# The 8x8 blocks' substitution on GpSimd, and the v and z projections among the quarters of S5's outputs

## The chip, the cores and the metric

The kernel runs on one core of a Trainium2 chip. The metric is the device time of one execution in microseconds (us), as the median of several runs. The engines are TensorE (PE; its weight loads are listed as PEld), VectorE (DVE), ScalarE (ACT), GpSimd (POOL) and SyncE (SP), which issues the weight transfers. Each engine works through its own queue of instructions in order.

## The reference

A two-layer decoder trunk over 16 meta tokens and 256 tokens (272 columns here), model width 1024, all in float32. In each layer

```
h += 1/2 * SwiGLU(RMSNorm(h))
h += Mixer(RMSNorm(h))
h += 1/2 * SwiGLU(RMSNorm(h))
```

The mixer has one input projection whose columns go to three groups: stick-breaking attention (q, k, v, 256 columns each, 4 heads of 64), gated DeltaNet (its own qkv of 768 columns, a gate z of 256, and the small b and a), and S5 (512 columns, u).

```
o_sb = rmsnorm(stick_breaking(q, k, v)) 
o_dn = rmsnorm(chunk_gated_delta_rule(...), out_norm) * silu(z)
y    = gelu(S5 states and inputs through C, D);  y = y * sigmoid(y @ w_glu + b_glu)
o_s5 = rmsnorm(y)
out  = concatenate([o_sb, o_dn, o_s5]) @ w_out
```

The delta rule works in chunks of 64 tokens and needs, for each chunk and head, the inverse of a unit lower triangular 64 x 64 matrix (`triangular_solve` of lmat + eye against eye).

## The kernel before, in words

Activations are kept transposed: channels on the 128 partitions, tokens along the free axis. Every large product is done three times to keep float32 accuracy: values are split into a high part rounded for TensorE and a low part (`xh`, `xl` and, for weights, `wh`, `wl`), and `mm3` (lines 142 to 146) issues high x high, high x low, low x high.

Weights come in units. `weights` (line 127) starts the transfer of a unit of up to 128 x 1088 into a buffer `raw` (3 buffers), ScalarE rounds it into `wh` (line 136), and VectorE, or GpSimd where the unit's number within the mixer is in `ON_POOL` (line 47), subtracts to get `wl` (line 139). `unit` (line 1306) projects 128 columns of the mixer's input: 8 blocks of 128 rows x 3 = 24 products into one PSUM tile, which VectorE evicts with the norm factor R (`proj`, line 1361).

The mixer (line 1317) writes its steps down in the order of `ORD` (line 41), after two convolution units, the DeltaNet gates and inverse, and the four u units. The letters: c is the other four convolution units, z the z projection with its Silu and gain, s S5's scan, r the rest of DeltaNet, q the projections of q, k and v, g S5's outputs and the GLU, b the attention, m and n norms. After `ORD` come the output projection's parts in the order `WOUT`.

The order in which each engine's queue is filled is not the written order: the tile framework plans it. It simulates the program with a cost for every instruction and takes instructions that are ready by priority; `high_priority(n)` moves a step ahead by n places (`FIRST` = 4000 for DeltaNet, `SECOND` = 1500 for S5's outputs, the GLU and their norm). Buffers of one tag (PSUM tags a, b, c, d with two buffers each) are handed on in the written order. `order` adds an edge without a semaphore between two instructions of a queue; `phase` and `act` use it to keep the activations of one table set together. The sets follow each other as Silu, exp/log, Silu, Gelu with Tanh, exp/log in each mixer.

The parts that the change touches:
- `dn_inverse` (line 970) inverts the triangular blocks in levels. Nine groups of 8 x 8 blocks (`Lb`, `TT8`) are solved by forward substitution on VectorE: for j = 0 to 6 a product (line 1005) and a subtraction (line 1006) on the columns that are left, 9 x (7 - j) elements per partition, each depending on the one before. Then the result is spread to 32 x 32 (line 1008), transposed on VectorE (line 1010), and joined on TensorE in rounds of small products: px and py for 16 and 32 (lines 1016 to 1025), px and py again for 64 and 128 (lines 1033 to 1071), with VectorE and ScalarE copying in between.
- `s5` (line 802) works in four quarters: products into PSUM (pinc, tag b), rotations and two scans on VectorE, one-column memsets on GpSimd.
- `s5_outputs` (line 842) works in the same four quarters: 24 small products each into one tile pY (tag b; lines 850 and 852), and four Gelu activations of 32 partitions.
- `do_z` projects z, applies Silu, and multiplies by the DeltaNet output gain `dng` (line 1373). `dn_out` (line 1185) multiplies the DeltaNet output by it and splits the product (lines 1201, 1202).
- `sb` (line 1205) first transposes v (pvs, PSUM tag c, line 1216), then takes its score tiles pz from the same tag.

Of the kernel before, what the change touches and what calls it, by code (L numbers as in the profile page):

```python
# [39 lines left out]
SBP = 0  # L40
ORD = "czsrqgbmn"
WOUT = "SnY"
# [3 lines left out]
CONV, UORD, ZK = (0, 1, 4, 5), (0, 1, 2, 3), 0  # L46
ON_POOL = (5, 7, 10, 15, 20, 25)
NBUF = (3, 2, 3)
# [15 lines left out]
class Trunk:  # L64
    def __init__(self, ctx, tc, a, out):
        self.ctx, self.tc, self.nc, self.a, self.out = ctx, tc, tc.nc, a, out
        pool = lambda n, b, **k: ctx.enter_context(tc.tile_pool(name=n, bufs=b, **k))
        self.const = pool("const", 1)
        self.res = pool("res", 1)
        self.raw = pool("raw", NBUF[2])  # L70
        self.wsp = pool("wsp", 2)
        self.small = pool("small", 1)
        self.ps = pool("ps", 1, space=PSUM)
        self.load_ins, self.set = None, None
        self.first = []
        self.since = []
        self.nw = 0
        self.on_pool = ()
        self.blocks = (0, 4)


# [60 lines left out]
    def mm3(self, p, wh, wl, xh, xl, first, last):  # L142
        mm = self.nc.tensor.matmul
        mm(p, wh, xh, start=first, stop=False)  # L144
        mm(p, wh, xl, start=False, stop=False)  # L145
        mm(p, wl, xh, start=False, stop=last)  # L146
# [126 lines left out]
    def load_params(self, prm):  # L273
# [26 lines left out]

        for t in (self.s5g, self.bglu):
            nc.vector.tensor_scalar(t, t, 0.5, None, op0=ALU.mult)
        self.dng = g("dn_out_norm", pat="p (l b) -> p l b", l=DEPTH)
        self.sbg = g("sb_out_norm", pat="p (l b) -> p l b", l=DEPTH)
# [536 lines left out]

    def s5_outputs(self, u):

        A, PE = self.nc.scalar, self.nc.tensor
        for r in range(4):
            p = self.psum("b", "pY")
            for b in range(4):
                q = 4 * b + r
                po = p[:, b * NCH:(b + 1) * NCH]
                PE.matmul(po, self.M0[:, q, :], self.U[:, r, b, :], start=True, stop=False)  # L850
                for k in range(2):
                    PE.matmul(po, self.W2[k][:, q].rearrange("p k g c -> p (k g c)"), self.S[r][:, k, b], start=False, stop=k == 1)  # L852
            for t in range(4):
                o = u[32 * r:32 * r + 32, :, t * NCH:t * NCH + NCH]
                self.act(o, p[32 * t:32 * t + 32, :T].rearrange("p (b c) -> p b c", b=4), AF.Gelu_apprx_tanh)

# [113 lines left out]
    def dn_inverse(self):  # L970
# [213 lines left out]

    def dn_out(self, zg, slot):

# [5 lines left out]
        for b in range(2):  # L1192
# [124 lines left out]
    def mixer(self, l, nxt):  # L1317
# [9 lines left out]
        with ExitStack() as es:  # L1327
# [32 lines left out]

            def proj(c0, dst):
                for b in range(2):
                    p, = self.unit(w_in[:, c0 + b * P:c0 + b * P + P], P)
                    V.scalar_tensor_tensor(dst[:, b, :], p[:, :T], 0.125 if c0 == 0 else 1.0, R, op0=ALU.mult, op1=ALU.mult)

            q, k, v = (tmp.tile([P, 2, T], F32, name=f"p{n}") for n in "qkv")

            def do_z():
                proj(1536, zr)
                self.phase(SET_SILU)  # L1370
                for b in range(2):
# [39 lines left out]

            steps = dict(z=do_z, s=do_s5, r=do_rest, q=do_qkv, b=do_sb, c=do_conv, g=do_glu, n=do_norm, m=do_r5)
            for x in ORD:
# [25 lines left out]
            for x in WOUT:  # L1439
                if x == "n":  # L1440
                    with first():
                        self.dn_out(zr, 2)
                    continue
# [51 lines left out]
```

## Time and profile before

| | |
|---|---|
| median of 3 runs | 1191.51 us (1189.88 to 1191.59) |
| the profiled execution | 1194.31 us |
| its span, from the first to the last instruction | 1192.5 us |
| mean granted clock of TensorE | 0.972 of full speed |
| TensorE products | 9544, busy 97% of the span |
| VectorE, ScalarE, GpSimd | busy 72%, 52%, 15% |

The rows further down are from this one execution. Times in them count from the span's start. A product's end is modelled, so products overlap in the list and a busy TensorE may still wait inside; the granted clock is 1.00 at 2.4 GHz and 0.50 at 1.2 GHz. Spans on GpSimd are rough. "Idle before" names what ended an engine's wait.

### The profile page before, as it was taken

Reading aid. Unit: us, or ns where it says so; the run is one execution under the profiler, and the core shown is the slowest. Engines: PE = TensorE matmul, PEld = TensorE weight load, DVE = VectorE, ACT = ScalarE, POOL = GpSimd, SP = SyncE. Lnnn points to the kernel's source line nnn. Section 1 sums busy time; section 2 is a strip of 40 time slices with the busy share of each in tenths; the row PEclk is TensorE's granted clock in tenths of the full one; section 3 lists DMA queues with packets and bytes.
Section 4 is the critical chain, followed back from the end, with each engine's and each line's share of the span. In section 5 each row is a group of like instructions: output and inputs, shape, how many; then the busy total and the mean of one; then the engine's idle time right before and its main releaser. Section 6 shows DMA issues by size and latency. Waiting matters only on the chain.

```text
span 1192.5 us, 23762 instructions
## 1 busy us (share of the span) xinstructions
PE 1154.8 (97%) x9544; PEld 1104.5 (93%) x9544; DVE 853.6 (72%) x1648; ACT 614.1 (52%) x981; POOL 175.3 (15%) x210
## 2 busy tenths in 40 slices
PE   8999999999998999999999999999999989999997
PEld 7999999998786999999999999999988969999985
DVE  7999986699636866555579998756994268666644
ACT  6455575564166654444455556645632566555533
POOL 6312100021010111110201112011210001111100
PEclk9999999999789999999999999999997599999999
DMA  5656545543201455555565555455431015666663
GB/s 182 179 175 180 166 135 160 167 125 108 71 19 54 142 175 177 168 176 171 177 187 177 169 173 172 132 175 156 124 112 33 27 45 185 181 188 191 187 191 117
DMA packets 196858, 173.74 MB, mean 146 GB/s; under 512 B 21300, under 2 KB 193004, under 8 KB 196748
## 3 DMA queue, kind: packets, MB, share of 16 engines
q1 hardware_dynamic: 196732, 172.22, 48.2%
q8 instruction: 75, 1.23, 0.4%
q14 instruction: 35, 0.29, 0.1%
q10 hardware_dynamic: 16, 0.00, 0.0%
HBM read 171.15 MB, written 1.05 MB: 144 GB/s over the span
## 4 chain that ended last, share of the span: by engine, by line
PE 84%; DVE 10%; ACT 3%; issue 1%; DMA 1%; SPq 0%; ACTq 0%; DVEq 0%
PE proj L146 17%; PE proj L145 17%; PE proj L144 17%; PE pd L146 5%; PE pd L145 5%; PE pd L144 5%; PE pd L493 5%; DVE wl L139 2%; PE pY L852 1%; DVE qkv L1346 1%; DVE xT L1437 1%; PE pY L850 1%; PE pl L887 1%; PE pm L783 1%; PE pz L1227 1%
## 5 line engine op out<-in xcount | busy, mean ns | idle before, releaser
L144 PE MATMUL proj<-xh,wh 128*128 128x272 f32 (+1 forms) x1840 | 521.1, 289 | 6.3 <-DVE sy L1435 2.8
L145 PE MATMUL proj<-xl,wh 128*128 128x272 f32 (+1 forms) x1840 | 518.4, 287 | 0.2 <-DVE xl L1296 0.2
L146 PE MATMUL proj<-xh,wl 128*128 128x272 f32 (+1 forms) x1840 | 492.8, 290 | 3.3 <-DVE wl L139 3.0
L136 ACT ACTIVATE wh<-raw 128x1024 fp32r<-128x1024 f32 (+1 forms) x324 | 338.2, 1044 | 292.8 <-PE proj L145 99.5
L139 DVE TENSOR_TENSOR wl<-raw,wh 128x1024 fp32r<-128x1024 f32 (+1 forms) x312 | 378.4, 1213 | 146.6 <-PE pd L146 60.9
L144 PEld LDWEIGHTS proj<-xh,wh 128*128 128x128 f32 x1840 | 345.4, 188 | 10.5 <-DVE sy L1435 4.1
L145 PEld LDWEIGHTS proj<-xl,wh 128*128 128x128 f32 x1840 | 345.2, 188 | 3.0 <-issue 1.5
L146 PEld LDWEIGHTS proj<-xh,wl 128*128 128x128 f32 x1840 | 328.8, 187 | 7.2 <-DVE wl L139 5.8
L144 PE MATMUL pd<-hh,wh 128*128 128x272 f32 x528 | 149.6, 288 | 0.0
L145 PE MATMUL pd<-hl,wh 128*128 128x272 f32 x528 | 149.3, 288 | 0.0
L435 POOL TENSOR_TENSOR hl<-h,hh 128x272 fp32r<-128x272 f32 (+1 forms) x88 | 81.1, 924 | 452.9 <-ACT hh L434 452.8
L146 PE MATMUL pd<-hh,wl 128*128 128x272 f32 x528 | 140.8, 288 | 0.2
L144 PEld LDWEIGHTS pd<-hh,wh 128*128 128x128 f32 x528 | 99.2, 188 | 0.2
L145 PEld LDWEIGHTS pd<-hl,wh 128*128 128x128 f32 x528 | 99.3, 188 | 0.1
L146 PEld LDWEIGHTS pd<-hh,wl 128*128 128x128 f32 x528 | 95.1, 188 | 1.0 <-DVE wl L139 0.9
L107 ACT ACTIVATE g<-g 128x272 f32<-128x272 f32 (+2 forms) x92 | 37.6, 415 | 68.9 <-DVE g L429 68.8
L433 DVE TENSOR_TENSOR h<-proj,g 128x272 f32<-128x272 f32 (+1 forms) x88 | 37.7, 433 | 32.9 <-PE proj L146 21.3
L434 ACT ACTIVATE hh<-h 128x272 fp32r<-128x272 f32 (+1 forms) x88 | 36.4, 419 | 47.1 <-DVE h L433 47.1
L429 DVE TENSOR_TENSOR g<-proj,R 128x272 f32<-128x272 f32 (+1 forms) x88 | 37.5, 430 | 17.8 <-PE proj L146 17.6
L139 POOL TENSOR_TENSOR wl<-raw,wh 128x1024 fp32r<-128x1024 f32 x12 | 30.7, 2557 | 110.5 <-ACT th L107 34.9
L431 DVE TENSOR_TENSOR g<-g,R 128x272 f32<-128x272 f32 (+1 forms) x88 | 37.7, 432 | 12.6 <-ACT g L107 12.3
L376 POOL TENSOR_TENSOR acc<-acc,sq 128x272 f32<-128x272 f32 (+1 forms) x20 | 22.7, 1134 | 91.4 <-ACT sq L370 90.5
(490 smaller groups left out, 1310.1 us busy)
## 6 DMA issues: line engine op xcount, KB each, us to landing
raw<-in_ffn_w_gate_dram SPq DMA_DIRECT2D x88, 512.0 KB, 3.6
raw<-in_ffn_w_up_dram SPq DMA_DIRECT2D x88, 512.0 KB, 3.6
raw<-in_ffn_w_down_dram SPq DMA_DIRECT2D x70, 512.0 KB, 3.5
raw<-in_w_in_dram SPq DMA_DIRECT2D x36, 512.0 KB, 4.4
raw<-in_ffn_w_down_dram SPq DMA_DIRECT2D x24, 384.0 KB, 3.0
raw<-in_w_out_dram SPq DMA_DIRECT2D x16, 512.0 KB, 3.5
raw<-in_s_w_glu_dram SPq DMA_DIRECT2D x4, 512.0 KB, 3.4
xin<-in_x_dram SPq DMA_DIRECT2D x4, 256.0 KB, 5.8
```

The costliest lines, as they stand in the source:

```text
L107: i = self.nc.scalar.activation(out, in_, func, **k)
L136: nc.scalar.activation(h[:, :n], r[:, :n], AF.Copy)
L139: e.tensor_tensor(l[:, :n], r[:, :n], f32(h[:, :n]), op=ALU.subtract)
L144: mm(p, wh, xh, start=first, stop=False)
L145: mm(p, wh, xl, start=False, stop=False)
L146: mm(p, wl, xh, start=False, stop=last)
L429: V.tensor_tensor(g1, pg[j][:, :N], R, op=ALU.mult)
L431: V.tensor_tensor(g1, g1, R, op=ALU.mult)
L433: V.tensor_tensor(h, pu[j][:, :N], g1, op=ALU.mult)
L434: nc.scalar.activation(hh[:, f, :N], h, AF.Copy)
L435: G.tensor_tensor(hl[:, f, :N], h, f32(hh[:, f, :N]), op=ALU.subtract)
L493: PE.matmul(pd[i][e], x[:, f, ts], w[:, 0, e * 512:e * 512 + 512], start=f == 0 and w is h and x is hh, stop=f == NF - 1 and w is lo)
```

## The change

- In the inverse the copy of the identity into `TT8`, the fourteen instructions of the substitution and the spread to 32 x 32 are issued on GpSimd instead of VectorE. The transpose behind them stays on VectorE.
- The steps z and v leave their places. z is no longer a letter of `ORD`, and `do_qkv` projects q and k only. S5's outputs are written as quarter 0, unit v0, quarter 1, unit v1, quarter 2, unit z0, quarter 3, unit z1, then the GLU. An order edge (`behind`) puts the first product of each unit behind the last product of the quarter before it; nothing binds the next quarter behind the unit but the written order.
- z's Silu becomes a Tanh of half the argument (in the Gelu set) and one VectorE instruction, (tanh + 1) * z. The missing half is put into the gain, which is halved at the start and applied in `dn_out`, as the scale of the rounding activation and in the subtraction.
- `ON_POOL` loses the numbers 10 and 15, which were the first z unit and the second k unit. The other four numbers stand for the same units as before (the last u, the second convolution of step c, the first and the last-but-two of the output projection).

```
-ORD = "czsrqgbmn"
+ORD = "csrqgbmn"
-ON_POOL = (5, 7, 10, 15, 20, 25)
+ON_POOL = (5, 7, 20, 25)
...
     def mm3(self, p, wh, wl, xh, xl, first, last):
         mm = self.nc.tensor.matmul
-        mm(p, wh, xh, start=first, stop=False)
+        i = mm(p, wh, xh, start=first, stop=False)
+        if self.behind is not None:
+            self.order(getattr(i, "ins", i), self.behind)
+            self.behind = None
...
-        for t in (self.s5g, self.bglu):
+        self.dng = g("dn_out_norm", pat="p (l b) -> p l b", l=DEPTH)
+        for t in (self.s5g, self.bglu, self.dng):
             nc.vector.tensor_scalar(t, t, 0.5, None, op0=ALU.mult)
...
-    def s5_outputs(self, u):
+    def s5_outputs(self, u, r):
...
-        V.tensor_copy(TT8, bc(self.id8, 1, 9))
+        G.tensor_copy(TT8, bc(self.id8, 1, 9))
         for j in range(7):
-            V.tensor_tensor(t8[:, :, j + 1:], Lb[:, :, j + 1:, j], TT8[:, :, j:j + 1].to_broadcast([P, 9, 7 - j]), op=ALU.mult)
-            V.tensor_tensor(TT8[:, :, j + 1:], TT8[:, :, j + 1:], t8[:, :, j + 1:], op=ALU.subtract)
+            G.tensor_tensor(t8[:, :, j + 1:], Lb[:, :, j + 1:, j], TT8[:, :, j:j + 1].to_broadcast([P, 9, 7 - j]), op=ALU.mult)
+            G.tensor_tensor(TT8[:, :, j + 1:], TT8[:, :, j + 1:], t8[:, :, j + 1:], op=ALU.subtract)
         TT32, T32 = t9("TT32"), t9("T32")
-        V.tensor_tensor(TT32.rearrange("p u (b i) -> p u b i", b=4), bc(TT8, 2, 4),
+        G.tensor_tensor(TT32.rearrange("p u (b i) -> p u b i", b=4), bc(TT8, 2, 4),
...
-            A.activation(self.xh[:, slot + b, :], y, AF.Copy)
-            V.tensor_tensor(self.xl[:, slot + b, :], y, f32(self.xh[:, slot + b, :]), op=ALU.subtract)
+            A.activation(self.xh[:, slot + b, :], y, AF.Copy, scale=g)
+            V.scalar_tensor_tensor(self.xl[:, slot + b, :], y, g, f32(self.xh[:, slot + b, :]), op0=ALU.mult, op1=ALU.subtract)
...
-            def do_z():
-                proj(1536, zr)
-                self.phase(SET_SILU)
-                for b in range(2):
-                    self.act(zr[:, b, :], zr[:, b, :], AF.Silu)
-                    V.tensor_scalar(zr[:, b, :], zr[:, b, :], self.dng[:, l], None, op0=ALU.mult)
+            def do_z(b):
+                proj(1536, zr, b)
+                t = self.cv("zt")[:, :T]
+                self.act(t, zr[:, b, :], AF.Tanh, scale=0.5)
+                V.scalar_tensor_tensor(zr[:, b, :], t, 1.0, zr[:, b, :], op0=ALU.add, op1=ALU.mult)
...
-                for c0, dst in ((0, q), (256, k), (512, v)):
-                    proj(c0, dst)
+                for c0, dst in ((0, q), (256, k)):
+                    for b in range(2):
+                        proj(c0, dst, b)
...
-                    self.s5_outputs(u)
+                    units = (proj, 512, v, 0), (proj, 512, v, 1), (do_z, 0), (do_z, 1)
+                    for r, (f, *args) in enumerate(units):
+                        self.behind = self.s5_outputs(u, r)
+                        f(*args)
                     self.acc = self.glu(l, u)
```

`s5_outputs(u, r)` is the body of the old loop for one r, and returns its last product.

## Rows read from the trace of the kernel before

**Rows 1.** The page: busy time of each engine; TensorE's clock in 40 slices.
```profile
PE 1154.8 (97%) x9544; PEld 1104.5 (93%) x9544; DVE 853.6 (72%) x1648; ACT 614.1 (52%) x981; POOL 175.3 (15%) x210
...
PEclk9999999999789999999999999999997599999999
```

**Rows 2.** Stretches: length, busy (count) of PE, PEld, DVE, ACT, POOL; PEclk, DMA share, GB/s.
```profile
265.00:308.10 43.10, 38.89 (x307) 36.42 (x305) 42.85 (x88) 16.60 (x26) 7.77 (x7) 0.99 0.41 122
...
308.10:325.00 16.90, 16.86 (x292) 13.99 (x292) 9.07 (x20) 1.06 (x4) 0.11 (x1) 0.51 0.10 33
...
325.00:341.80 16.80, 16.80 (x301) 16.24 (x295) 2.91 (x7) 7.66 (x20) 2.55 (x5) 1.00 0.01 3
...
341.80:349.70 7.90, 7.06 (x37) 6.73 (x35) 1.92 (x5) 3.33 (x10) 0.63 (x1) 0.57 0.00 0
...
357.80:389.00 31.20, 27.29 (x199) 21.01 (x200) 20.57 (x55) 18.29 (x39) 0.44 (x1) 1.00 0.16 51
...
420.00:840.00 420.00, 419.49 (x3361) 415.57 (x3360) 298.51 (x535) 218.54 (x320) 58.97 (x66) 1.00 0.57 171
...
912.30:931.20 18.90, 18.90 (x233) 18.28 (x226) 3.04 (x7) 6.94 (x18) 1.38 (x4) 0.85 0.01 2
...
931.20:949.80 18.60, 18.17 (x90) 17.24 (x90) 5.00 (x14) 8.91 (x20) 2.35 (x1) 0.51 0.09 29
...
952.40:982.00 29.60, 25.47 (x192) 19.71 (x193) 19.09 (x50) 18.41 (x39) 0.29 (x1) 1.00 0.16 54
```

**Rows 3.** VectorE by form, 265 to 308.1 us: busy us, mean ns, idle before.
```profile
L139 DVE TENSOR_TENSOR wl<-raw,wh 128x1024 fp32r<-128x1024 f32 x8 | 9.7, 1211 | 0.0
...
L1364 DVE SCALAR_TENSOR_TENSOR pz<-proj,R 128x272 f32<-128x272 f32 x2 | 0.8, 422 | 0.0
...
L1373 DVE TENSOR_SCALAR pz<-pz,prm 128x272 f32<-128x272 f32 x2 | 0.7, 342 | 0.0
...
L1008 DVE TENSOR_TENSOR TT<-TT,m8c 128x288 f32<-128x288 f32 x1 | 0.5, 452 | 0.0
```

**Rows 4.** VectorE in order of time: start, us, instruction.
```profile
265.17 2.95 DVE L1346 SCALAR_TENSOR_TENSOR qkv<-pad,prm,qkv 128x272 f32<-128x272 f32 x2
...
268.73 0.49 DVE L1346 SCALAR_TENSOR_TENSOR qkv<-pad,prm,qkv 128x272 f32<-128x272 f32 x1
...
283.46 0.23 DVE L1005 TENSOR_TENSOR t<-Lb,TT 128x63 f32<-128x63 f32 x1
...
288.08 1.64 DVE L1006 TENSOR_TENSOR TT<-TT,t 128x54 f32<-128x54 f32 x1
...
308.61 0.47 DVE L1010 STREAM_TRANSPOSE T<-TT 128x288 f32<-128x288 f32 x1
```

**Rows 5.** Line 1005 alone, 265 to 308.1 us: length, VectorE busy (count).
```profile
265.00:308.10 43.10, 1.39 (x7) 0.99 0.41 122
```

**Rows 6.** Line 1006 alone, the same stretch.
```profile
265.00:308.10 43.10, 2.74 (x7) 0.99 0.41 122
```

**Rows 7.** GpSimd in order of time: start, us, instruction.
```profile
264.91 2.37 POOL L139 TENSOR_TENSOR wl<-raw,wh 128x1024 fp32r<-128x1024 f32 x1 [3.25 <-PE proj L146]
...
273.93 2.05 POOL L1001 TENSOR_TENSOR Lm<-L,lev 128x288 f32<-128x288 f32 x2 [6.65 <-ACT qkv L1344]
...
286.55 3.10 POOL L139 TENSOR_TENSOR wl<-raw,wh 128x1024 fp32r<-128x1024 f32 x1 [1.42 <-PE proj L146]
```

**Rows 8.** Tile px in two stretches: length, busy of PE, PEld, DVE, ACT.
```profile
308.10:325.00 16.90, 2.31 (x144) 2.06 (x144) 0.00 (x0) 0.43 (x2) 0.51 0.10 33
...
325.00:341.80 16.80, 2.85 (x64) 2.59 (x64) 0.86 (x2) 1.09 (x3) 1.00 0.01 3
```

**Rows 9.** Tile py, 325 to 341.8 us: the same columns.
```profile
325.00:341.80 16.80, 2.78 (x134) 2.56 (x135) 1.30 (x3) 0.37 (x1) 1.00 0.01 3
```

**Rows 10.** Tile pz, 308.1 to 325 us: the same columns.
```profile
308.10:325.00 16.90, 4.58 (x18) 2.58 (x12) 0.00 (x0) 0.00 (x0) 0.51 0.10 33
```

**Rows 11.** Tile pY, 325 to 341.8 us: length, busy of PE, PEld, ACT.
```profile
325.00:341.80 16.80, 11.79 (x96) 11.09 (x96) 5.40 (x14) 1.00 0.01 3
```

More of the change, by code (lines that the diff above doesn't have):

```diff
@@ L143, in mm3 @@
         mm = self.nc.tensor.matmul
-        mm(p, wh, xh, start=first, stop=False)
+        i = mm(p, wh, xh, start=first, stop=False)
+        if self.behind is not None:
+            self.order(getattr(i, "ins", i), self.behind)
+            self.behind = None
         mm(p, wh, xl, start=False, stop=False)
@@ L299, in load_params @@
         self.cw = g("dn_conv_w", pat="p (l k b) -> p l k b", l=DEPTH, k=4)
-        for t in (self.s5g, self.bglu):
+        self.dng = g("dn_out_norm", pat="p (l b) -> p l b", l=DEPTH)
+        for t in (self.s5g, self.bglu, self.dng):
             nc.vector.tensor_scalar(t, t, 0.5, None, op0=ALU.mult)
-        self.dng = g("dn_out_norm", pat="p (l b) -> p l b", l=DEPTH)
         self.sbg = g("sb_out_norm", pat="p (l b) -> p l b", l=DEPTH)
@@ L840, in s5 @@
             self.S.append(z)
-    def s5_outputs(self, u):
[L844 to L855, printed above, removed]
+    def s5_outputs(self, u, r):
+        PE = self.nc.tensor
+        p = self.psum("b", "pY")
+        for b in range(4):
+            q = 4 * b + r
+            po = p[:, b * NCH:(b + 1) * NCH]
+            PE.matmul(po, self.M0[:, q, :], self.U[:, r, b, :], start=True, stop=False)
+            for k in range(2):
+                i = PE.matmul(po, self.W2[k][:, q].rearrange("p k g c -> p (k g c)"), self.S[r][:, k, b], start=False, stop=k == 1)
+        for t in range(4):
+            o = u[32 * r:32 * r + 32, :, t * NCH:t * NCH + NCH]
+            self.act(o, p[32 * t:32 * t + 32, :T].rearrange("p (b c) -> p b c", b=4), AF.Gelu_apprx_tanh)
+        return getattr(i, "ins", i)
     def dn_tile(self, sh, nm, b=1):
@@ L1183, in dn_norm, with dn_out @@
         V.tensor_tensor(o, o, bc(r, 2, 64), op=ALU.mult)
-    def dn_out(self, zg, slot):
+    def dn_out(self, zg, g, slot):
         nc = self.nc
@@ L1359, in mixer, with proj @@
             zr = tmp.tile([P, 2, T], F32, name="pz")
-            def proj(c0, dst):
-                for b in range(2):
-                    p, = self.unit(w_in[:, c0 + b * P:c0 + b * P + P], P)
-                    V.scalar_tensor_tensor(dst[:, b, :], p[:, :T], 0.125 if c0 == 0 else 1.0, R, op0=ALU.mult, op1=ALU.mult)
+            def proj(c0, dst, b):
+                p, = self.unit(w_in[:, c0 + b * P:c0 + b * P + P], P)
+                V.scalar_tensor_tensor(dst[:, b, :], p[:, :T], 0.125 if c0 == 0 else 1.0, R, op0=ALU.mult, op1=ALU.mult)
             q, k, v = (tmp.tile([P, 2, T], F32, name=f"p{n}") for n in "qkv")
-            def do_z():
-                proj(1536, zr)
-                self.phase(SET_SILU)
-                for b in range(2):
-                    self.act(zr[:, b, :], zr[:, b, :], AF.Silu)
-                    V.tensor_scalar(zr[:, b, :], zr[:, b, :], self.dng[:, l], None, op0=ALU.mult)
+            def do_z(b):
[3 more added lines that the diff above has]
+                V.scalar_tensor_tensor(zr[:, b, :], t, 1.0, zr[:, b, :], op0=ALU.add, op1=ALU.mult)
             def do_s5():
@@ L1410, in do_r5 @@
                     self.rms(self.acc, 4 * 512, 0, self.R5, "b")
-            steps = dict(z=do_z, s=do_s5, r=do_rest, q=do_qkv, b=do_sb, c=do_conv, g=do_glu, n=do_norm, m=do_r5)
+            steps = dict(s=do_s5, r=do_rest, q=do_qkv, b=do_sb, c=do_conv, g=do_glu, n=do_norm, m=do_r5)
             for x in ORD:
@@ L1441, in mixer @@
                     with first():
-                        self.dn_out(zr, 2)
+                        self.dn_out(zr, self.dng[:, l], 2)
                     continue
```

## The prediction

> **What bounds the kernel now.** I read the page first, then the two mixers by stretches, then each engine inside the stretches. On the page TensorE (PE) is busy 97% of the span, and its granted clock is full except in slices that fall in the mixers, one per layer [rows 1]. In the feed-forward stretch from 420 to 840 us there is nothing to win: 3361 products in 419.5 us at full clock, 0.125 us each, so a projection unit of 24 products costs 3.0 us [rows 2]. What can be won lies in the mixers. Layer 1's VectorE order repeats layer 0's some 588 us later, so I work layer 0 out and give layer 1's differences. Four stretches matter [rows 2]:
> S1, 265.0 to 308.1 us: VectorE is busy 42.85 of 43.1 us, TensorE stands for 4.2. VectorE is the bound.
> S2, 308.1 to 325.0: TensorE is busy throughout, but at a granted clock of 0.51, after the idle time at the end of S1; here run DeltaNet's small products, the inverse's first rounds (tiles px, py) and the attention scores (pz).
> S3, 325.0 to 341.8: TensorE is full; S5's four quarters (pY) and the rest of the inverse.
> S4, from 341.8: the GLU's products, at a clock of 0.57 over 7.9 us; in layer 1 S3 runs at 0.85 and S4 at 0.51 over 18.6 us.
> After S4's last Tanh ScalarE loads the exp/log table and the attention chain runs, 31.2 us in layer 0 and 29.6 in layer 1 [rows 2]. Its end lets the last output projection start, so time taken out before the table load is won, as long as that chain keeps its length.
>
> **The change, part by part, per layer.** Instructions on VectorE start about 0.08 us closer together than they last, so I take 0.08 off each that goes.
>
> VectorE in S1, what goes. The substitution's 14 instructions last 1.39 + 2.74 us [rows 5, 6], but one of the latter lasts 1.64 [rows 4] where its neighbours last 0.2; without that excess (1.44) they are 2.7. The initial copy is 0.2 and the masked spread 0.45 [rows 3]: 3.4 together. The excess goes too. It is a hold: the slow instruction, started at 288.08, ends at 289.72, and GpSimd's 3.10 us subtraction from 286.55 ends at 289.65 [rows 4, 7]. The other subtraction that leaves GpSimd does the same: two convolution steps take 2.95 us from 265.17, beside GpSimd's from 264.91, where one alone takes 0.49 [rows 4, 7]; 2.0 us. So 3.4 us of holds go. Three low-part subtractions (z1, v0, v1) move out, one (k1, on GpSimd before) comes in: 2 x 1.21 = 2.4. Four evictions at 0.42 and two gain multiplications at 0.34 go: 2.4 [rows 3]. Sum 11.6, less 24 x 0.08 = 1.9: 9.7 us.
>
> VectorE in S1, what comes. GpSimd's sixteen instructions (copy, 14, spread) hold VectorE whenever it reads two operands from SBUF. The nearest rows for one: 1.03 us for 288 elements and 2.37 for 1024 [rows 7], so an estimate of 0.50 fixed and 1.8 ns an element. The 14 have 504 elements together: 7.0 + 0.9 = 7.9; copy and spread make it 9.6 us. VectorE pays between nothing (when each falls beside an instruction that reads PSUM) and 9.6; I take half, 4.8, since the two rows on holds show a part of GpSimd's time held in one and nearly all in the other. Also, the substitution took from 283.46 until its transpose at 308.61 [rows 4], 25 us, because its links are scattered in VectorE's queue. On GpSimd, 16 instructions of 0.6 with a wait of about as much before each take some 19 us at most, and they start about 4 us earlier, as z's work ahead of them is gone. So the inverse begins 10 us or more earlier, and of its nine VectorE steps (0.45 each by the spread's row) more than half come into S1: 2.5. S1: -9.7 + 4.8 + 2.5 = -2.4 us, with -9.7 and +2.4 as ends. TensorE is no bound there: 38.9 us of work less four units of 3.0 leaves 27, in about 41.
>
> TensorE in S2. The inverse's first rounds (px 2.31 us [rows 8]) find room in S1's idle time, and the scores (4.58 us [rows 10]) wait now: their PSUM buffers come after v's transposes, and v comes later. -6.9.
>
> TensorE in S3. v0, v1 and z0 come in, 9.0 us. The scores follow at full clock, 2.3. Of the inverse's 2.85 + 2.78 us here [rows 8, 9] I let half go; later DeltaNet steps take the other places: -2.6. pY's 11.79 us stay [rows 11]. +8.7. ScalarE and VectorE, busy 7.7 and 2.9 of 16.8 us here [rows 2], hide the units' copies, subtractions, evictions and z's Tanh. If ScalarE's cover is gone (its Gelus stand behind copies that wait for a weight buffer), a quarter's Gelu comes up to one unit, 3.0 us, later. The weight transfers move with the units and pass nothing on SyncE's queue but the GLU's and output's weights, which come later; DMA is 1% busy in S3, so they cost nothing. The new order edge binds a unit's first product behind its quarter's last, on one queue; behind that product stand the next quarter and the GLU (through its PSUM buffers), and they wait only if the unit's low part is late, which VectorE's idle 13.9 us hide. S5's one-column memsets on GpSimd now stand among the substitution's instructions: one of 0.6 us is the most that each should wait, and pY needs them much later.
>
> S4. z1 comes in, 3.0, into the 0.84 us in which TensorE waits for the last Gelus. The quarters now alternate with dense units, so I expect full clock up to the GLU: that gives back (1 - 0.57) x 7.9 = 3.4 in layer 0, and 9.1 in S4 plus 2.8 in S3 in layer 1 [rows 2]. S4: -1.2 in layer 0; in layer 1 (gap 0.43) 2.6 - 9.1 - 2.8 = -9.3.
>
> The tail. Layer 1's attention chain is 1.6 us shorter than layer 0's, and its DeltaNet is further ahead when the table is loaded; so -1.6 in layer 0, nothing in layer 1. The gain folded into the output (two VectorE instructions and two activations with a scale) costs about 0.2: a scalar form with a per-partition operand lasts 0.49 against 0.42 [rows 3, 4]. It could be 0.5.
>
> Sum: layer 0 -2.4 - 6.9 + 8.7 - 1.2 - 1.4 = -3.2; layer 1 -2.4 - 6.9 + 8.7 - 9.3 + 0.2 = -9.7. Together -12.9 on the profiled execution's 1194.3 us, 1181.4; that execution is 2.8 above the median of 1191.5, so 1178.6, in round figures 1179.
>
> **Rivals.**
> A, more: GpSimd's instructions fall where VectorE reads PSUM (4.8 us less per layer), and TensorE runs the 10 us left of S2 at full clock (4.9 less). Fully that is -32 us; half of it, a further 10, gives 1169. For it: half of S2's low-clock products leave. Against: S2 keeps only small products, and S1 now leaves TensorE idle for some 14 us instead of 4.2 right ahead of it.
> B, the holds eat it: VectorE stands for all of GpSimd's 9.6 us; 2 x 4.8 more makes 1188. If the transpose on VectorE stands early in its queue and waits for GpSimd (behind it are S5's scans and the units' subtractions, and TensorE waits for these), another 4 us per layer makes 1196. For it: the 1.64 us row. Against: a waiting VectorE holds nothing, so GpSimd then runs freely.
> The Trainium skill ("SBUF — State Buffer", section "Who interferes with whom") states the hold as a rule: GpSimd and VectorE share one port pair under an exclusive lock, kept for a whole instruction. By that rule this rival has its full 9.6 us; the 289.65 and 289.72 us above agree with it.
> C, slower: v and z run at the low clock. Place: S3 and S4. All four units then cost 6.0 instead of 3.0 (+12 per layer), and the credits of 3.4 and 11.9 are lost: 12.9 is answered by +39.3 over both layers. It decides from a third of that on (13 us); at half, the time is 1198. For it: layer 1's S4 stayed at 0.51 through 18.6 us although the GLU's dense products fill most of it. Against: S3 came to full clock in layer 0 with pY alone.
>
> **How the numbers follow.** My forecast (1172 to 1187) gets 0.48, A 0.20, B 0.15, C 0.17. The range reaches half-way into A and to C's half: 1166 to 1197. About 0.2%, 2.4 us, is what a measurement tells from no change. Faster: all but 0.02 of the forecast, all of A, 0.07 of B: 0.73. Same: 0.01 of the forecast, 0.04 of B and 0.03 of C: 0.08. Slower: the rest, 0.19.
>
> **What would show it.** In S1: no substitution on VectorE, its instructions on GpSimd at about 0.6 us each, and VectorE instructions of 0.2 to 0.7 us stretched by as much beside them (B if most are). S5's last scan in each layer 2 to 3 us earlier; the transpose (line 1010 before) by 10 or more. TensorE's first pY about 9 us earlier than 325, and the quarters with units between them at a clock of 1.0 (C if 0.5). The GLU's products at 0.126 us apart in both layers, and the exp/log table loaded 2 us earlier in layer 0, some 10 in layer 1. The prediction is wrong if the table load of layer 0 is later than before, or if layer 1 gains no more than layer 0.

## The result, and the profile after

The changed kernel takes 1210.52 us (median of 4, 1210.11 to 1211.47) against 1190.70 us of the kernel before (median of 4): ratio 1.0172, interval 1.0152 to 1.0191. It is 20 us slower where I forecast 12 faster, and outside my range. The profiled execution took 1210.34 us, its span is 1208.5, 16.0 more than before. The ratios here and below leave out slow executions, over 1.5% above the fastest of their kernel (one of e7, three of e12, one of e13).

The page after, beside [rows 1]: TensorE's busy time rose by 10.8 us with the same 9544 products, so products got longer, not more. In the clock's row layer 0's mixer shows 8, 5 where 7, 8 stood.
```profile
PE 1165.6 (96%) x9544; PEld 1114.7 (92%) x9544; DVE 854.4 (71%) x1621; ACT 614.1 (51%) x981; POOL 181.7 (15%) x238
...
PEclk9999999998598999999999999999976989999998
```

Layer 0's mixer after by stretches, and layer 1's last three (columns as in [rows 2]); the mixer, counted from the last Newton step of its norm, starts at 234.6 and 835.1 us where it was 236.1 and 824.1.
```profile
262.00:287.00 25.00, 24.79 (x203) 23.52 (x201) 24.79 (x49) 11.89 (x19) 6.50 (x12) 1.00 0.46 127
287.00:291.30 4.30, 0.04 (x4) 0.07 (x6) 2.74 (x6) 0.00 (x0) 3.14 (x7) 0.93 0.38 122
291.30:303.30 12.00, 9.78 (x250) 9.29 (x251) 11.62 (x24) 0.80 (x2) 0.22 (x2) 0.50 0.01 3
303.30:313.40 10.10, 10.10 (x192) 8.84 (x191) 6.73 (x17) 1.17 (x3) 1.49 (x5) 0.50 0.02 4
313.40:328.50 15.10, 15.10 (x92) 14.59 (x91) 1.27 (x3) 2.29 (x6) 0.00 (x0) 0.51 0.00 0
328.50:353.80 25.30, 25.30 (x238) 24.40 (x236) 9.67 (x22) 11.50 (x25) 1.81 (x1) 1.00 0.19 63
353.80:368.60 14.80, 13.02 (x103) 10.40 (x101) 10.15 (x18) 10.12 (x21) 2.35 (x1) 1.00 0.23 72
...
914.00:926.00 12.00, 12.00 (x74) 11.70 (x71) 1.27 (x3) 2.29 (x6) 0.00 (x0) 0.52 0.00 1
926.00:953.00 27.00, 27.00 (x257) 25.95 (x255) 9.67 (x22) 11.49 (x25) 0.00 (x0) 1.00 0.20 59
953.00:967.80 14.80, 12.96 (x103) 10.38 (x101) 10.14 (x18) 10.12 (x21) 2.35 (x1) 1.00 0.23 71
```
Read them from the top. At 287 q's and k's units are through, and TensorE stands for 4.3 us: v's and z's products, which filled this place before, are gone. From 291 to 328.5 the clock is 0.50, 37 us long where the stretch at 308 to 325 was 17 [rows 2]; TensorE is busy nearly all of it. The quarters (313.4 to 353.8) take 40.4 us where 16.8 stood [rows 2]. Only while v's first unit runs does the clock come back. The GLU then has full clock in both layers, as forecast.

The product that ends the idle time, TensorE's order after:
```profile
291.26 0.97 PE L1022 MATMUL px<-T,Lm 32*32 32x32 f32 x55 [4.27 <-DVE T L1016]
```

The substitution on GpSimd, some of its sixteen, and VectorE beside it (start, us):
```profile
281.92 0.35 POOL L1011 TENSOR_TENSOR t<-Lb,TT 128x63 f32<-128x63 f32 x1 [0.15 <-ACT Lb L1002]
...
282.83 1.19 POOL L1011 TENSOR_TENSOR t<-Lb,TT 128x54 f32<-128x54 f32 x1
284.10 0.31 POOL L1012 TENSOR_TENSOR TT<-TT,t 128x54 f32<-128x54 f32 x1
...
289.82 0.79 POOL L1014 TENSOR_TENSOR TT<-TT,m8c 128x288 f32<-128x288 f32 x1
```
```profile
282.49 1.34 DVE L141 TENSOR_TENSOR wl<-raw,wh 128x1024 fp32r<-128x1024 f32 x1
...
290.64 0.48 DVE L1016 STREAM_TRANSPOSE T<-TT 128x288 f32<-128x288 f32 x1 [1.53 <-POOL TT L1014]
...
301.96 1.34 DVE L837 TENSOR_TENSOR_SCAN s5z<-dec,s5z 128x272 f32<-128x272 f32 x2
```
This part went better than I thought: 281.92 to 290.61, 0.3 us an instruction where nothing is in the way. It is GpSimd that waits: its 1.19 us instruction starts while VectorE's subtraction of 282.49 runs and ends 0.2 us after it; that subtraction is 0.13 us over the mean of [rows 3], and the most that another VectorE instruction beside the sixteen is stretched is 0.16 (the one at 281.98). The last scan ends at 303.3 (311.9 before), the transpose is at 290.64 (308.61 in [rows 4]).

ScalarE's load of the exp/log table in the two layers, which I had named as the test, before and after:
```profile
357.82 1.28 ACT L97 ACT_TABLE_LOAD   x1
...
952.45 1.28 ACT L97 ACT_TABLE_LOAD   x1
```
```profile
368.55 1.28 ACT L99 ACT_TABLE_LOAD   x1
...
967.75 1.28 ACT L99 ACT_TABLE_LOAD   x1
```
In layer 0 that is 10.7 us later than before, 12.2 counted from the mixer's start.

### The profile page after: what moved, and what is told of

It reads as the page before. It is cut to its first block, busy times and chain, and to the rows that moved or that the text cites. A ratio compares the mean times of both kernels' runs of the same rounds, so it can differ in the third digit from the quotient of the medians.

```text
span 1208.5 us, 23745 instructions
## 1 busy us (share of the span) xinstructions
PE 1165.6 (96%) x9544; PEld 1114.7 (92%) x9544; DVE 854.4 (71%) x1621; ACT 614.1 (51%) x981; POOL 181.7 (15%) x238
## 4 chain that ended last, share of the span: by engine, by line
PE 88%; DVE 6%; ACT 3%; POOL 1%; issue 1%; DMA 1%; SPq 0%; ACTq 0%; DVEq 0%; POOLq 0%
PE proj L151 18%; PE proj L146 18%; PE proj L150 18%; PE pd L151 5%; PE pd L150 5%; PE pd L146 5%; PE pd L498 5%; PE pY L856 2%; DVE wl L141 1%; PE pl L892 1%; PE pY L854 1%; PE pm L788 1%; POOL TT L1012 1%; PE pz L1248 1%; POOL t L1011 1%
## 5 line engine op out<-in xcount | busy, mean ns | idle before, releaser
L141 DVE TENSOR_TENSOR wl<-raw,wh 128x1024 fp32r<-128x1024 f32 (+1 forms) x316 | 383.8, 1215 | 155.9 <-PE pd L151 59.6
L146 PEld LDWEIGHTS proj<-xh,wh 128*128 128x128 f32 x1840 | 349.4, 190 | 14.0 <-DVE sy L1445 4.8
L150 PEld LDWEIGHTS proj<-xl,wh 128*128 128x128 f32 x1840 | 349.1, 190 | 5.3 <-DVE xl L1302 2.0
L151 PEld LDWEIGHTS proj<-xh,wl 128*128 128x128 f32 x1840 | 332.6, 190 | 5.3 <-DVE wl L141 3.0
L434 DVE TENSOR_TENSOR g<-proj,R 128x272 f32<-128x272 f32 (+1 forms) x88 | 37.5, 430 | 17.9 <-PE proj L151 17.8
L141 POOL TENSOR_TENSOR wl<-raw,wh 128x1024 fp32r<-128x1024 f32 x8 | 20.3, 2538 | 157.7 <-PE proj L151 65.1
```

The source lines that it names most:

```text
L141: e.tensor_tensor(l[:, :n], r[:, :n], f32(h[:, :n]), op=ALU.subtract)
L146: i = mm(p, wh, xh, start=first, stop=False)
L434: V.tensor_tensor(g1, pg[j][:, :N], R, op=ALU.mult)
```

## The experiments

**Theories.** After the two traces I held theory 1: taking the dense units out of the scans' stretch lets TensorE idle, its clock falls there and stays low. Theory 2: whatever the clock, DeltaNet's later steps (first in priority) and four units now stand ahead of the GLU. Theory 3: the substitution on GpSimd costs by itself. For each kernel the table gives the time, and, as "lost", the sum over pieces of 2 us of both mixers (262 to 430 and 850 to 1030 us) of 2 us x (1 - granted clock) in its profiled execution: the time that full clock would save if TensorE were busy and the bound throughout. The ratios are against executions of the kernel before on the same chip (medians 1189.2 to 1190.7).

| kernel | median us (executions) | ratio to before, 95% | profiled us | lost us |
|---|---|---|---|---|
| before | 1190.7 (4) | 1 | 1194.3 | 30.7 |
| changed | 1210.5 (4) | 1.0172 [1.0152, 1.0191] | 1210.3 | 44.4 |
| e1 substitution alone | 1222.1 (4) | 1.0243 [1.0193, 1.0293] | 1223.1 | 61.4 |
| e2 moves alone | 1193.9 (10) | 1.0029 [1.0002, 1.0056] | 1194.6 | 27.3 |
| e3 changed, filled behind k | 1205.9 (10) | 1.0108 [1.0073, 1.0143] | 1206.9 | 34.1 |
| e4 changed, v back | 1207.7 (4) | 1.0127 [1.0078, 1.0177] | 1208.0 | 46.1 |
| e5 changed, rounds held | 1195.0 (10) | 1.0036 [1.0011, 1.0061] | 1195.3 | 27.3 |
| e6 v back, z ahead | 1200.0 (10) | 1.0076 [1.0040, 1.0112] | 1207.9 | 44.4 |
| e7 e1, filled late | 1194.5 (10) | 1.0020 [0.9977, 1.0063] | 1190.5 | 18.8 |
| e8 units one quarter ahead | 1209.7 (4) | 1.0134 [1.0072, 1.0197] | 1211.7 | 42.7 |
| e9 rounds held, v back | 1192.0 (12) | 1.0006 [0.9981, 1.0031] | 1189.1 | 32.4 |
| e10 e5, filled | 1196.4 (12) | 1.0046 [1.0027, 1.0065] | 1197.5 | 15.3 |
| e11 before, filled | 1182.4 (12) | 0.9942 [0.9915, 0.9969] | 1182.6 | 11.9 |
| e12 e1, filled thrice | 1194.8 (12) | 0.9974 [0.9929, 1.0020] | 1215.7 | 44.4 |
| e13 e9, filled thrice | 1180.3 (7) | 0.9910 [0.9876, 0.9944] | 1179.1 | 6.8 |
| e14 e9, filled at the GLU | 1184.9 (12) | 0.9960 [0.9933, 0.9986] | 1184.9 | 23.9 |
| e15 e1, little rounds again | 1232.8 (4) | 1.0357 [1.0305, 1.0409] | 1232.5 | 70.0 |

**e1, the substitution alone** (kernel before; on GpSimd also the copy and the spread).
```
-ON_POOL = (5, 7, 10, 15, 20, 25)
+ON_POOL = (5, 7, 20, 25)
-            V.tensor_tensor(t8[:, :, j + 1:], ...)
+            G.tensor_tensor(t8[:, :, j + 1:], ...)
```


> The kernel before with the substitution of the 8x8 blocks on GpSimd (and the wl tiles divided as in the changed kernel), the v and z projections at their old places in do_qkv. Theory 1 (the loss is TensorE's clock: four dense units taken out of the scans' stretch leave TensorE idle at 287 to 291 us, its clock falls there and stays at 0.50 for 37 us): the dense units stand between the inverse's rounds as before, the clock falls no earlier than at the last scan, and the time is 1176 to 1190 us, most likely 1183. Theory 2 (the quarters' stretch is longer because DeltaNet's later steps come ahead of the Gelu, whatever the clock): the transpose comes early here too, so the later steps come early too: 1190 to 1200 us. Theory 3 (the substitution on GpSimd itself costs, by holding VectorE up or by ending late): 1195 us or more.


1222.1 us: slower than the whole change. Theory 1 as put is out: here the dense units are in their old places. Three stretches (columns as in [rows 2]):
```profile
285.00:310.00 25.00, 23.32 (x450) 22.01 (x449) 23.41 (x44) 6.10 (x8) 7.92 (x18) 1.00 0.34 107
310.00:345.00 35.00, 34.78 (x262) 30.71 (x262) 9.21 (x22) 6.79 (x18) 2.09 (x5) 0.51 0.05 16
345.00:375.00 30.00, 29.54 (x184) 27.08 (x182) 9.90 (x24) 12.33 (x27) 4.20 (x2) 0.61 0.06 18
```
The clock falls at 311 us, later than before, and then stays at 0.50 until 368, though TensorE stands for only 0.22 us of the middle stretch. So it isn't the place of the fall that costs here, but how late the clock comes back. The inverse's first four rounds (72 records of px or py each), of which three ran within the low stretch before, now run at full clock ahead of it.

**e2, the moves alone** (the changed kernel; V for G in all sixteen).
```
-            G.tensor_tensor(t8[:, :, j + 1:], ...)
+            V.tensor_tensor(t8[:, :, j + 1:], ...)
```


> The changed kernel with the substitution back on VectorE, the v and z projections behind the quarters. Theories 1 and 2 (the moved units cost the time): 1205 to 1215 us, as slow as the changed kernel; the clock falls at about 290 us and stays low until v's products. Theory 3 (the substitution on GpSimd costs it): 1195 us or less.


1193.9 us, as theory 3 wants. The clock falls at 291 us as in the changed kernel, but is back by 311, as two stretches show:
```profile
302.70:311.00 8.30, 8.30 (x219) 7.33 (x222) 5.99 (x16) 0.40 (x1) 0.11 (x1) 0.50 0.02 4
311.00:340.00 29.00, 29.00 (x443) 27.95 (x436) 8.66 (x16) 11.54 (x26) 1.45 (x5) 1.00 0.15 48
```

**e3, filled behind k.** Products that nothing reads, of k's weights, 48 in each mixer.
```
+                for i in range(2):
+                    for j in range(NB):
+                        self.mm3(pf[:, :T], h[:, j, :], lo[:, j, :], self.xh[:, j, :], self.xl[:, j, :], ...)
```


> The changed kernel with 48 more dense products of k's kind in each mixer, which are computed behind k's projection and read by nothing, no part of the result changed: some 6 us more of TensorE's work in each layer, put where its clock fell. Theory 1: the clock falls later, the loss by low clock between 290 and 330 us goes from 18.7 us to under 12 in layer 0, and the time is below 1206 us in spite of the 12 us of added work. Theory 2: the clock makes no difference to the end, 1210 to 1216 us. Theory 3: 1210 or more.


1205.9: 4.6 us less with 12 us more work. The clock falls at 299 in place of 291; in 290 to 330 us it loses 12.0 against 18.7, right at the bound of theory 1, and the time is just below its 1206.

**e4, v back** (z behind quarters 2 and 3).
```
-                for c0, dst in ((0, q), (256, k)):
+                for c0, dst in ((0, q), (256, k), (512, v)):
```


> The changed kernel with v's two dense units back in do_qkv and only z's two behind the quarters. Theory 1: half of the dense work is back among the scans, the clock falls later than 291 us and the quarters' stretch is shorter by v's 6 us: 1188 to 1200 us. Theory 2: the quarters are shorter by v's 6 us in each layer only where nothing else fills them: 1198 to 1206. Theory 3: no better than 1205.


1207.7: missed by theory 1. The fall comes at 304, and the clock is back only at 344, when z's unit runs: v's products, used up early, are missing later.

From these four I formed theory 4: a kernel's time is nearly the same work at full clock plus the time lost at 0.50, and what counts is whether work that brings the clock back stands where it has fallen. The held rounds test it against theory 3.

**e5, the rounds held**: the first product of px behind the last norm product.
```
+        self.order(self.px0, self.pn_last)
```


> The changed kernel with the first product of the inverse's rounds held in TensorE's queue behind the last norm product, so that the rounds run behind the scans as they do with the substitution on VectorE; the substitution stays on GpSimd. Theory 3 (the substitution on GpSimd itself costs, by holds or by its own length): 1203 us or more. Theory 4 (what costs is only that the early transpose lets the inverse's rounds run out before the clock falls or while TensorE idles, so that they don't lift it again in the quarters' stretch; a kernel's time is some 1160 us at full clock plus the time lost at 0.50): the clock is back by 315 us in layer 0, the loss by low clock is as with the substitution on VectorE, and the time is 1187 to 1198 us.


1195.0 us with the substitution still on GpSimd: theory 3 is out, and one order edge takes 15.5 us off the changed kernel. Two stretches:
```profile
302.50:311.00 8.50, 8.50 (x253) 7.50 (x252) 5.74 (x13) 0.80 (x2) 0.11 (x1) 0.52 0.01 3
311.00:340.00 29.00, 29.00 (x403) 27.99 (x403) 9.06 (x17) 11.42 (x26) 1.83 (x5) 1.00 0.16 52
```
These are e2's rows nearly to the digit: with the inverse's first three rounds (px, py) behind 302.5 the clock returns at 311; in the changed kernel, where only later rounds stand there, at 328.5. The low stretch ahead of 302 costs little, since VectorE is the bound there.

**e6, z ahead** (v in `do_qkv`; the loop of e8 below with these units).
```
+                    units = ((do_z, 0),), ((do_z, 1),), (), ()
```


> v's units in do_qkv among the scans, z's first unit behind the last norm product and ahead of the first quarter of S5's outputs, z's second behind that quarter; all else as in the changed kernel. Theory 4: the clock falls near 304 us as in the kernel with v back, but z's dense products come at once and it is back by about 316 us in place of 344; the time is 1168 to 1184 us, faster than the kernel before. Theory 2 (the work ahead of the Gelu's end decides, whatever the clock): z only changes places with the quarters, 1203 to 1210 us. Theory 3: 1203 us or more.


Missed: 1200.0. z0's 24 dense products were spread among the inverse's little ones from 310.7 to 321.9, and the clock came back at 334, not 316. But its ten executions are the plainest sight of what low clock costs: same instructions, spans from 1193.1 us at a mean clock of 0.972, over 1198.2 at 0.968, to 1206.6 at 0.960. Span times clock is 1158 to 1162 in all ten.

**e7, e1 filled late.** The same 48 products as in e3, with v's weights, behind the last norm product.
```
+                            if i == j == 0:
+                                self.order(self.fill0, self.pn_last)
```


> The kernel before with the substitution on GpSimd (1222 us), and behind the last norm product of each mixer 48 more dense products with v's weights, which nothing reads: 12 us more of TensorE's work at full clock, no part of the result changed. Theory 4: these products bring the clock back before the first quarter, 27 us less is lost at 0.50 in each mixer, and the time falls to 1178 to 1196 us in spite of the added work. Theories 2 and 3: the added work adds its 12 us or more, 1230 to 1240 us.


1194.5: 28 us less than e1 with 12 us more work. Theory 2 is out as the cause of e1's time. Two of these products, in order of time (start, us):
```profile
315.28 0.43 PE L147 MATMUL pfill<-xl,wh 128*128 128x272 f32 x1
...
317.08 0.29 PE L145 MATMUL pfill<-xh,wh 128*128 128x272 f32 x1
```
The time of one goes from 0.43 to 0.29 us at 316, where e1 stayed low to 368. That is the profiled execution; the ten run from 1188.7 to 1207.6 us, the clock's mean from 0.983 to 0.966.

**e8, each unit one quarter ahead.**
```
+                    i = self.pn_last
+                    for r in range(4):
+                        for f, *args in units[r]:
+                            self.behind = i
+                            f(*args)
+                        i = self.s5_outputs(u, r)
```


> The changed kernel with each of the four dense units one quarter earlier: v's first ahead of the first quarter, z's second ahead of the last. The same work on every engine. Theory 4: the clock falls at 291 us as before, v's products are there some 10 us earlier, and it is back by about 314 us in place of 328: 1186 to 1198 us. Theory 2: no work is removed from ahead of the table load, 1206 to 1212 us. Theory 3: 1206 to 1212 us.


1209.7, missed. Layer 0 did as theory 4 says (back at 315, 15.4 us lost in 280 to 390 in place of 22.2); in layer 1 the clock came back at 911 for a few us, fell again and stayed low until 932. The same order gave two courses, so a place for v and z alone doesn't settle the clock.

**e9, rounds held and v back**, v behind the third set of S5's input products.
```
+                self.behind = self.pinc[2]
+                proj(512, v, 0)
+                proj(512, v, 1)
```


> The changed kernel with the rounds held behind the last norm product, v's two dense units back in do_qkv behind the third set of S5's input products, where TensorE stood idle for 7.2 us, and z's units behind the last two quarters. Theory 4 (the time is some 1160 us at full clock plus what is lost at 0.50): TensorE has dense work to about 294 us, the clock falls some 8 us later than with the rounds held alone and the rounds bring it back at the same place; 4 to 8 us lost in each mixer in place of 12 to 14, the time 1174 to 1186 us. Rival (the rounds bring the clock back only because of what stands beside them, and without v's units in the first quarters it falls again): 1192 to 1206 us.


1192.0, at the edge of the rival: the fall goes to 297, nearly as expected, but the clock is back at 318 and not at 311, and a new fall stands behind the GLU (942 to 956 us in layer 1).

**e10, e5 filled.** From here on the unread products are of xh with itself (`self.fill(n, behind)`), which hold no weight buffer.
```
+                self.fill(48, self.pinc[2])
+                self.fill(24, self.pinc[3])
```


> The changed kernel with the rounds held, and 72 dense products of xh with itself which nothing reads (48 behind the third set of S5's input products, 24 behind the fourth) in each mixer, in TensorE's idle stretches of 7.2 and 2.3 us; no part of the result changed. Theory 4, and that it is the idle stretch at 287 to 302 us that lets the clock fall: no fall at 291 us, some 10 us less lost in each mixer, the time 1172 to 1184 us, faster than the kernel before. Rival (the clock falls at the next slack, a few us later, and the products only add work): 1192 to 1202 us.


The rival's: 1196.4. The fall moves from 290 to 302, the clock returns at 312 (311 in e5), and the 12 us of low clock that went had cost nothing, since TensorE waited for VectorE in them: the last scan ends at 303.7, no earlier than in e5 (302.9). So "lost" is an upper limit: it counts only where TensorE is the bound.

**e11, the kernel before, filled.**
```
+                self.fill(24, self.pinc[3])
...
                     self.s5_outputs(u)
+                    self.fill(24, self.pY_last)
```


> The kernel before with 48 such unread products in each mixer: 24 behind the fourth set of S5's input products (TensorE's slack at 304 to 308 us) and 24 behind the last quarter of S5's outputs, ahead of the Gelu's projections. No part of the result changed. Theory 4: one or both of the two falls in each mixer (30.8 us lost in all) go or get shorter, against 6 to 12 us of added work: 1172 to 1188 us. Rival: the falls come a few us later with the same length, 1194 to 1204 us.


1182.4, 0.6% faster than before: 48 products a mixer that nobody needs make the tuned kernel faster. The fall at 308 comes at 312 and is 10 us long in place of 17; that ahead of the GLU (342 to 349 in layer 0, 925 to 949 in layer 1) goes. Two stretches of layer 0:
```profile
310.00:345.00 35.00, 35.00 (x617) 32.34 (x617) 12.02 (x27) 11.29 (x30) 3.30 (x6) 0.85 0.01 2
345.00:375.00 30.00, 28.41 (x229) 23.29 (x228) 17.61 (x37) 22.52 (x45) 2.38 (x1) 1.00 0.22 71
```

**e12, e1 filled thrice** (e11's two and, ahead of the quarters, a third).
```
+                    self.fill(24, self.pn_last)
```


> The kernel before with the substitution on GpSimd (1222 us) and 72 such unread products in each mixer: 24 behind the fourth set of S5's input products, 24 behind the last norm product, 24 behind the last quarter. No part of the result changed. Theory 4: the long stretch at 0.50 (310 to 368 us) goes but for a few us, and the time is 1172 to 1192 us with 18 us of added work. Theory 3 is out already; the rival is that the products ahead of the quarters lift the clock only for a short time: 1200 to 1230 us.


Inconclusive: its executions run from 1180.7 us to 1217.4, at mean clocks of 0.993 down to 0.961, and the profiled one is among the long ones. The filling holds the clock in some executions and not in others.

**e13 and e14, e9 filled**: 24 products behind the GLU's last (e14); in e13 also 24 behind v's last and 24 behind the fourth input set.
```
+            if c:
+                self.fill(24, self.mm_last)
```


> The kernel with the rounds held and v back (1192 us; span times clock 1152 us), and 72 dense products in each mixer that nothing reads: 24 behind v's last product, 24 behind the fourth set of S5's input products, 24 behind the last Gelu projection. No part of the result changed. Theory 4: the falls at 296 and at 354 us (layer 1: 885 and 942) go or become short; some 6 of the 9 us added stand in idle time: 1164 to 1180 us, below the filled kernel before (1182), which would show that the change is worth some 10 us once the clock is kept. Rival (the falls only move some us later, as they did with the rounds held and filled): 1186 to 1200 us.

> The same with only the 24 products behind the last Gelu projection. Theory 4: the fall behind the Gelu's projections (354 us; 942 us, 13 us long) goes, the one among the scans stays: 1178 to 1190 us. Rival: 1190 to 1198 us.


e14 within its range: 1184.9, 7 us less than e9 by the medians, 5.5 by the ratios, whose intervals touch. The stretch behind the GLU in layer 1, first e9, then e14:
```profile
938.00:956.00 18.00, 16.57 (x100) 13.09 (x99) 12.03 (x27) 14.10 (x25) 0.00 (x0) 0.62 0.27 89
```
```profile
938.00:956.00 18.00, 18.00 (x155) 15.28 (x154) 13.62 (x31) 16.05 (x31) 0.29 (x1) 1.00 0.27 89
```
In e9 TensorE stood 1.4 us there, waiting for VectorE; filled, the clock stays. e13 has 1180.3 (just above the top of the forecast), 0.9% faster than before and the fastest here, though its interval overlaps that of e11. Its clock:
```profile
PEclk9999999999989999999999999999999999999998
```
So with the clock mostly kept the change in this form is worth 2 us (4 by the ratios) against the filled kernel before, not the 10 that I gave it; as the intervals overlap, and the two weren't timed side by side, it isn't shown to be worth anything.

**e15, little rounds again.** In e1, three rounds of 32 unread 32 x 32 products behind the last norm product.
```
+                                j = self.nc.tensor.matmul(p[s, g * 32:g * 32 + 32], self.LT[s, g, s], self.LT[s, g, s], start=True, stop=True)
```


> The kernel before with the substitution on GpSimd (1222 us), and in each mixer three rounds of 32 little products (32x32 on 32x32) that nothing reads, behind the last norm product, where that kernel stays at 0.50 from 310 to 368 us. No part of the result changed. If little products in close order bring the clock back (theory 4 as put for the rounds held): 1185 to 1205 us. If only dense products do, or if it was their place next to the pl and pv products: 1218 to 1230 us.


1232.8, above both: the clock stays at 0.50 from 307 to 370, in this stretch throughout.
```profile
310.00:345.00 35.00, 35.00 (x438) 31.61 (x436) 9.56 (x24) 4.76 (x13) 2.29 (x5) 0.50 0.04 12
```
Unread little products, here spread by the planner among others, didn't bring the clock back; dense ones did in e7, though not in e6. What in the held rounds' stretch (little rounds, gate products pl, transposes pv, close together) does it in e5, e2 and before stays open.

## Why the prediction was wrong, point by point

Two things make the difference: the clock, and products that now stand where TensorE is the bound. Between the profiled executions of before and after, 16.0 us apart, "lost" went up by 13.7, but that isn't what the clock cost: the low clock from 291 to 303 stands where VectorE is the bound, and that from 369 to 400 in the attention chain, whose length hardly changed (the tail below). So I count from the end of the last scan to the load of the exp/log table, where TensorE is busy 96 to 99% of the time: layer 0 and layer 1 before, after, and in e5 (columns as in [rows 2]).
```profile
311.94:357.82 45.88, 44.11 (x664) 40.47 (x662) 17.03 (x35) 18.81 (x44) 5.91 (x7) 0.79 0.05 14
899.12:952.45 53.33, 52.13 (x671) 47.75 (x670) 16.93 (x41) 19.29 (x44) 3.85 (x6) 0.66 0.04 12
```
```profile
303.30:368.55 65.25, 63.50 (x616) 58.20 (x615) 27.77 (x59) 25.03 (x54) 5.65 (x7) 0.81 0.13 42
903.95:967.75 63.80, 62.00 (x616) 56.84 (x615) 27.73 (x59) 25.03 (x53) 3.85 (x6) 0.83 0.14 42
```
```profile
302.94:360.65 57.71, 57.12 (x812) 52.57 (x800) 27.18 (x58) 25.11 (x54) 5.68 (x7) 0.93 0.15 47
894.80:953.23 58.43, 57.81 (x810) 53.00 (x800) 27.15 (x57) 25.11 (x54) 3.87 (x6) 0.92 0.15 47
```
Length times (1 - clock) gives what is lost here in both layers: 28 us before, 23 after, 9 in e5. TensorE's busy time less that is its work at full clock: 68, 102 and 106 us.

- Before and after: the stretches are 30 us longer. The clock took 5 us less in them, not more; the work is 34 us more, 24 of them the eight moved units. The last scans, which end 7.1 and 6.2 us earlier counted from the mixer's start, pay for 13 us.
- After and e5: the work is nearly the same (4 us more in e5), the clock gives back 15 us, and the profiled time falls by 15.0. One order edge does it, with all of the change's instructions in place; so 15 us of the changed kernel's time is low clock behind the scans, and not DeltaNet's later steps, which stand there in e5 too.
- Before and e5: with that clock back the changed kernel is still no faster than before (1.0036), where I had forecast 12 us. That part of the miss is work, not clock.

Over all kernels the profiled time runs from 1179 to 1232 us; less what is lost and less the unread products (0.125 us each), 1153 to 1169 is left. The 16 us that remain are as much as the change made, so this sum supports e5 and e7 but can't replace them. Theory 4 forecast the times of e5, e7, e11 and e14, missed e13 by a hair and e6, e8, e9, e10 and e15 outright: it says what low clock costs, not when the clock comes back.

Layer 0 / layer 1 by the prediction's stretches, counted from the mixer's start, forecast and measured:

| stretch | forecast | measured |
|---|---|---|
| S1, to the norm products | -2.4 / -2.4 | -6.0 / -6.0 |
| S2, to the first pY | -6.9 / -6.9 | -4.1 / -3.3 |
| S3, to the GLU | +8.7 / +5.9 | +22.3 / +17.9 |
| S4, to the table load | -1.2 / -6.5 | +0.1 / -4.3 |
| tail | -1.4 / +0.2 | -1.1 / +1.0 |
| sum | -3.2 / -9.7 | +11.2 / +5.3 |

(Layer 1's clock credit of 2.8 is put in S3 here, where it was to come.)

S1, mis-sized to the good side: I took 4.8 us of holds. It was GpSimd's instructions that waited, five of them, and no VectorE instruction beside them was stretched by more than 0.16 us. Rival B is out; e5, with all sixteen on GpSimd, is as fast as e2 with none. The Trainium skill ("SBUF — State Buffer", "Who interferes with whom") adds that issue order decides who blocks; the 1.19 us instruction, begun after VectorE's, agrees. What I overlooked is that a wait of 1.53 us for GpSimd's spread would now stand on VectorE, and behind it the 4.27 us on TensorE.

S2: right in kind, -4 in place of -7. The scores left, and so did px's first two rounds, but the inverse's next rounds came in their place: px and py together are busy 4.2 us in 303.0 to 313.4, where they were 3.5 us in 310.5 to 325.

S3, the step that failed. I let the quarters run at full clock with three units between them. Measured, in layer 0: four units, not three (+3.0); 15.1 us at 0.51, which is 7.4 lost; and DeltaNet's later steps, which the early inverse lets in here. TensorE's groups by form in 313.4 to 353.8 us (busy us, mean ns, idle before), two of them:
```profile
L1144 PE MATMUL pvn<-vb,TTf 128*128 128x64 f32 x8 | 1.2, 274 | 0.0
...
L1151 PE MATMUL pS<-ds,E 128*128 128x64 f32 x8 | 1.1, 281 | 0.0
```
These and their like (pvn, pS, pk of both chunks) are 6.8 us busy between 313.4 and 353.8. I had let half of the inverse leave and given DeltaNet's later steps no price beyond the places of the rest. The first and last of the three are work that moves, the middle one is the loss by the clock. They make 17.2 where the stretch missed by 13.6; of what went the other way, the scores' 2.3 us, which I had booked here, are a part.

S4: the credit for the GLU came in both layers (clock 1.00 over 353.8 to 368.6 and 953 to 967.8), and z1 stood in S3 already; but the scores (pz, 4.3 us busy), which I had booked in S3, stood in S4.

The account of S2 to S4, both layers: forecast -6.9 us, measured +28.6. I had booked 15.3 us given back by the clock, and some 5 came; the other 25 us of the miss of 35.5 are products that stand in these stretches and that I had priced too low or let leave. S1 came out 7 us better than forecast; the whole misses by 28.9 (-12.9 against +16.0). Of my rivals C had the sign, and the clock in S3; but three of the four units ran at full clock (the four are busy 15.8 us in S3, where C doubles their 12), and S4's credit came. The low clock stood in the stretch ahead of the units and was already there when they came. I had even written against A that S1 would leave TensorE idle for some 14 us right ahead of S2, and didn't draw the line on to S3. The fall came 17 us earlier than before and the return 4 us later.

My test held: "wrong if the table load of layer 0 is later than before". That layer 1 lost less than layer 0 (+5.3 against +11.2) is the part of the credit that was right.

## What to carry to other kernels

Before moving dense products out of a stretch, ask what TensorE will run there instead, and at which granted clock the work behind it will then run: a stretch of small products can stay at 0.50 for long (37 us in the changed kernel, 57 in e1), and the cost is paid far from the place of the change. Look for the fall and for the return separately; in e1 the return decided (a later fall, 57 us low). Count low clock only where TensorE is the bound, and price every product that moves from where another engine is the bound to where TensorE is: here 34 us against 13 won. Where TensorE waits for others, dense products that nobody reads can be worth their time (e11, e14; not e10), but check several executions: the same order held the clock in some and not in others (e6, e12).

## What the runs showed of the hardware

TensorE stayed at 0.50 while busy: for 34.78 of 35 us in e1 and for 35.00 of 35 in e15, over stretches of small products (S5's of 128 x 68 in f32 take the most time in them). The Trainium skill ("TensorE: Matmul & The Clock Gate", "What's actually happening") says that activity releases the throttle; e1 and e15 show TensorE busy for over 50 us, with gaps of under 1 us in all, without release. In e7 the clock came back among unread dense 128 x 272 products; in e6 24 such products, spread among little ones, went by without it. So in these runs being busy did not by itself bring the clock back; what did is open.

GpSimd's tensor_tensor of 9 to 63 elements a partition took 0.22 to 0.40 us when alone; I had estimated 0.5 to 0.6 from instructions of 288 and 1024.
